# Rotating straight from PSUM, and head pairs' logits in the two row halves of the array, in a two-layer encoder trunk

## The chip, the cores and the metric

The kernel runs on one NeuronCore of a Trainium2 chip. The metric is the device time of one execution in microseconds (us); the profiled times are counted from the first to the last instruction of that core (the span). TensorE (PE in the profile) multiplies, VectorE (DVE) and ScalarE (ACT) work elementwise, GpSimd (POOL) and SyncE (SP) here mostly issue DMAs.

## The reference, cut to what matters

Two layers act on a residual stream of 512 tokens by 1024 channels. Each has a SwiGLU block, a mixer, a second SwiGLU block and a gated embedding. The change lies in the mixer of layer 0, which has two attention groups over keys of the same or earlier chunks of 64 tokens:

```python
aq = apply_rope(rms_norm(aq.reshape(bsz, s_len, A_HEADS, HEAD_DIM), a_q_g), cos, sin)   # 8 heads
ak = apply_rope(rms_norm(ak, a_k_g)[:, :, None], cos, sin)[:, :, 0]
iq = apply_rope(iq.reshape(bsz, s_len, IDX_HEADS, IDX_DIM), cos, sin)                    # 4 index heads
ik = apply_rope(ik[:, :, None], cos, sin)[:, :, 0]
a_out = dsa_attention(aq, ak, av, iq, ik, iw, a_w_uv)     # the best 128 keys of each query, by index score
bq = apply_rope(rms_norm(bq...), cos, sin)                # 4 heads x 2 maps of 64 channels
bk = apply_rope(rms_norm(bk...), cos, sin)
b_out = diff_attention(bq, bk, bv, lam, subln_g, lam_init)  # softmax(map 0) - lam * softmax(map 1)

def apply_rope(x, cos, sin):
    x1, x2 = jnp.split(x, 2, axis=-1)
    return jnp.concatenate([x1 * c - x2 * s, x2 * c + x1 * s], axis=-1)
```

## The kernel before

Activations are kept transposed: a tile has 128 channels on its partitions and the 512 tokens along its free axis, so two heads of 64 channels share a tile. All weight products run as three matmuls of rounded halves (`mm3`, lines 281 to 283, type fp32r); the attention's own products of the second group run as plain fp32 (`mm`, line 276). One `mm` in fp32 is two MATMUL records in the trace, one in fp32r is one.

Instructions are not emitted in program order. Every helper hands `Plan` an engine, a cost in ns, a latency, the tiles it reads and writes, and a priority; `Plan.order` then simulates the engines greedily with these costs and with the number of slots of each pool (`SLOTS`, and `CAPS` for a stream's share; the pair `("ps", "lgpvB")` may hold 2 PSUM banks), and the kernel is emitted in the order that comes out. From there each engine works its list strictly in order and waits where an input is not there. A changed cost thus changes the order on every engine.

The mixer in layer 0 (`even_mixer`) runs from about 385 to 630 us of the span:

- 385 to 440: projections of the index heads and the shared key, rotation of three tiles, index scores (stream `sc`).
- 440 to 487: eight projections for `bqk` (four tiles of `bq`, four of `bk`), each rotated by `rope`; DVE starts to pick the best keys (`max` and `match_replace`, lines 912 and 913).
- 487 to 553: differential attention (stream `pvB`): for each of 4 heads and each of 4 query blocks `t` two logit products over N = 128 (t + 1) keys, then max, exponential, combination, transposes and the product with the values. The projections of `aq` (stream `aq`) fill the gaps on PE, each again rotated.
- 553 to 590: the output projection of that group (`down`), mixed with the start of the sparse attention; 590 to 630: the rest of the sparse attention (stream `pvA`).

`rope_` rotates a tile p (15 tiles in all: 3, then 8, then 4). ACT copies p out of PSUM to zc; four DMAs on SP's queue write the copy with each head's 32-channel halves exchanged to zs; DVE multiplies zc by cos and zs by sin (both with a gain per channel for 13 of the 15 tiles) and adds the two. `halves` makes two zeroed tiles for each `bk` tile (POOL memsets, line 343), into which DMAs put head map 0 in the upper and map 1 in the lower 64 partitions, so that a logit product can run over all 128 partitions with the whole `bq` tile.

Of the kernel before, what the change touches and what calls it, by code (L numbers as in the profile page):

```python
# [257 lines left out]
def trunk(ctx: ExitStack, tc: tile.TileContext, A: dict, out: bass.AP):  # L258
    nc = tc.nc
# [8 lines left out]
    def mm(p, a, b, start, stop):  # L268
        n = b.n
        if a.store.dt == F32R:  # L270
            cost = max(213.0 if n < 256 and n < 192 else 0.0, n * 0.422)
        else:
            cost = 150.0 if a.n <= 64 and n <= 128 else max(n, 127) * 1.68
            if a.arr.shape[0] <= 64:
                cost *= 2
        P.op("PE", cost, lambda: nc.tensor.matmul(ap(p), ap(a), ap(b), start=start, stop=stop), w=[p], r=[a, b], lat=160.0)  # L276

    def mm3(p, a, b, first, last):
# [82 lines left out]
    def tt(dt=F32, shape=(128, S)):  # L361
        return P.tile("t", shape, dt)
# [340 lines left out]
    def vectors():  # L703
        gdma(cst, A["cst"])
        qk = tt(shape=(4, 64))
        for i, name in enumerate(["b_q_g", "b_k_g", "a_q_g", "a_k_g"]):
            gdma(qk[i:i + 1, :], A[name])
        p = ps()
        for j in range(2):
            r = tt(shape=(4, 2, 2, 32))  # L710
            for b in range(2):
                for a in range(2):
                    vcopy(r[:, a, b, :], qk[:, 32 * (b ^ j):32 * (b ^ j) + 32])
            transpose(p[:, 4 * j:4 * j + 4], r.flat(), ident[0:4, 0:4])
        vcopy(vcol[:, 0:8], p[:, 0:8])
        vset(vcol[64:128, 3:4], 1.0)
        vset(vcol[64:128, 7:8], 1.0)
        vrow = tt(shape=(VR - 8, 128))
        gdma(vrow[0:1, :], A["b_subln_g"])
        gdma(vrow[1:9, :], A["c_b_s"][0])  # L720
        for i, name in enumerate(["d_conv_b", "d_ln_g", "d_ln_b"]):
            gdma(vrow[9 + 4 * i:13 + 4 * i, :], A[name].rearrange("e (k p) -> (e k) p", p=128))
        p = ps()
        transpose(p[:, 0:VR - 8], vrow, ident[0:VR - 8, 0:VR - 8])
        vcopy(vcol[:, 8:VR], p[:, 0:VR - 8])
        ts(vcol[:, 8:9], vcol[:, 8:9], 0.8, None, OP.mult)
# [46 lines left out]
    def even_mixer(norm, nxt, cos, sin):  # L773
# [8 lines left out]
                return rope_(*a)  # L782

        def rope_(p, gi, ssq=None):
            zc = tt()
            acopy(zc, p)
            if ssq is not None:
                sq = tt()
                act(sq, p, AF.Square)
                colsums(ssq, sq, ind)  # L790
            zs = tt()
            for b in range(4):
                dma(zs[32 * b:32 * b + 32, :], zc[32 * (b ^ 1):32 * (b ^ 1) + 32, :], 64)
            if gi is None:
                tmul(zc, zc, cos)
                tmul(zs, zs, sin)
            else:
                stt(zc, zc, vcol[:, gi:gi + 1], cos, OP.mult, OP.mult)
                stt(zs, zs, vcol[:, gi + 4:gi + 5], sin, OP.mult, OP.mult)
            dst = at()  # L800
            tadd(dst, zc, zs)
            return dst

        def head_factor(c, R):
# [8 lines left out]
        def stack(x, pool, both):  # L813

            hi, lo = split(x, tt)
            d = [[pool(F32R) for _ in range(2 if both else 1)] for _ in range(2)]
            for c in range(2):
                own = slice(64 * c, 64 * c + 64)
                for b in range(2):
                    half = slice(64 * b, 64 * b + 64)  # L820
                    if both:
                        dma(d[c][0].bitcast(F32)[half, :], hi.bitcast(F32)[own, :], 128)
                        dma(d[c][1].bitcast(F32)[half, :], lo.bitcast(F32)[own, :], 128)
                    else:
                        dma(d[c][0].bitcast(F32)[half, :], (hi, lo)[b].bitcast(F32)[own, :], 128)
            return d

        def halves():
            d = [at(), at()]
            gset(d[0][64:128, :], 0.0)  # L830
            gset(d[1][0:64, :], 0.0)
            return d

        wv = w.rearrange("(k p) c -> p k c", p=128)
# [99 lines left out]
        with P.on("side", SIDE_BIAS):  # L934
            fB = head_factor(rows, 16)
            fq = small(NT, 8)
            ts(fq, fB[:, :, 0:8], 0.125, None, OP.mult)
            bk = []
            for h in range(4):
                fb = bcast2(fB, 8 + 2 * h)  # L940
                d = halves()
                tmul(bqk[4 + h], fb, bqk[4 + h])
                for b in range(2):
                    dma(d[b][64 * b:64 * b + 64, :], bqk[4 + h][64 * b:64 * b + 64, :], 128)
                bk.append(d)

        P.stream = "main"

# [4 lines left out]
        def softmax_exp_(maps, N, bias, fcol):  # L953
            n = len(maps)
            mx, nb, sm = small(n), small(n), small(n)
            es = []
            for i, (q, ks) in enumerate(maps):
                p = ps()
                for j, k in enumerate(ks):
                    mm(p[:, 0:k.n], q, k, j == 0, j == len(ks) - 1)  # L960
                e = tt()
                dve(e[:, 0:N], lambda e=e, p=p, i=i: nc.vector.tensor_tensor_reduce(  # L962
                    out=ap(e[:, 0:N]), in0=ap(p[:, 0:N]), in1=ap(bias), scale=1.0, scalar=LOW,
                    op0=OP.add, op1=OP.max, accum_out=ap(mx[:, i:i + 1])), [p, bias], extra=[mx])
                es.append(e)
            stt(nb, mx, -1.0, fcol, OP.mult, OP.mult)
            for i, e in enumerate(es):
                act(e[:, 0:N], e[:, 0:N], AF.Exp, scale=fcol[:, i:i + 1], bias=nb[:, i:i + 1], accum=sm[:, i:i + 1])
            recip(sm, sm)
            return es, sm  # L970
# [17 lines left out]
        with P.on("pvB"):  # L988
            c = ps((128, NT, 4))
            oc = []  # L990
            for h in range(4):
                po = ps()
                for t in range(NT):
                    N = 128 * (t + 1)
                    (e0, e1), rs = softmax_exp([(bqk[h][:, 128 * t:128 * t + 128], (bk[h][c][:, 0:N],)) for c in range(2)],
                                               N, cmask[:, S - N:S], fq[:, t, 2 * h:2 * h + 2])
                    tmul(rs[:, 1:2], rs[:, 1:2], nlam)
                    scaled(e1[:, 0:N], e1[:, 0:N], rs[:, 1:2])
                    stt(e0[:, 0:N], e0[:, 0:N], rs[:, 0:1], e1[:, 0:N], OP.mult, OP.add)
                    pT = ps()  # L1000
                    for b in range(t + 1):
                        transpose(pT[:, 128 * b:128 * b + 128], e0[:, 128 * b:128 * b + 128], ident)
                    aT = tt()
                    moved(aT[:, 0:N], pT[:, 0:N])
                    for b in range(t + 1):
                        mm(po[:, 128 * t:128 * t + 128], bv[b][:, 128 * h:128 * h + 128],
                           aT[:, 128 * b:128 * b + 128], b == 0, b == t)
# [262 lines left out]
```

## Time and profile before

| what | value |
|---|---|
| median of 3 runs | 2010.78 us (2010.63 to 2011.23) |
| the profiled execution | 2010.54 us, span 2008.6 us |
| PE busy | 1991.3 us of the span, 99% |
| DVE busy / ACT busy / POOL busy | 1080.8 / 723.2 / 13.8 us |
| mean granted clock of PE | 0.999 of 2.4 GHz |

The difference of 1.9 us between time and span lies outside the instructions. A busy PE need not be at its full rate: matmuls overlap, and an instruction that starts late still counts as busy while its predecessor drains. So start times are compared below, not durations.

### The profile page before, as it was taken

The numbers are of one execution on the slowest core, as the hardware profiler recorded it, in microseconds if no ns is written. First come the engines' busy times: TensorE is split into PE (matmuls) and PEld (weight loads), VectorE is DVE, ScalarE is ACT, GpSimd is POOL, SyncE is SP. The second block draws the span as 40 slices with busy tenths as digits, with TensorE's granted clock in tenths as the row PEclk, the third lists the DMA queues.
The fourth block names the chain that finished last, engine by engine and source line by source line (L and its number), as shares of the span: only waits on it lengthen the run. The fifth ranks groups of instructions, "written<-read, shape, count | busy, mean of one in ns | idle before, by whom it ended". The sixth has DMA issues, their size and how long they took to land.

```text
span 2008.6 us, 22735 instructions
## 1 busy us (share of the span) xinstructions
PE 1991.3 (99%) x9154; PEld 1630.2 (81%) x9154; DVE 1080.8 (54%) x1797; ACT 723.2 (36%) x1057; POOL 13.8 (1%) x35
## 2 busy tenths in 40 slices
PE   8999999999999999999999999999999999999999
PEld 7888888888767888888888888888767888888887
DVE  6442464489986544344466443444699744334443
ACT  6322233344756422132254222223425533213232
POOL 0000000000000000000000000000000000000000
PEclk9999999999999999999999999999999999999999
DMA  5323322354330323332233322323333232323222
GB/s 189 105 97 98 108 85 84 94 160 141 96 110 22 104 86 105 94 95 95 95 121 110 105 98 92 105 75 103 107 105 105 84 97 92 105 85 104 95 104 75
DMA packets 164778, 202.28 MB, mean 101 GB/s; under 512 B 9968, under 2 KB 123072, under 8 KB 164672
## 3 DMA queue, kind: packets, MB, share of 16 engines
q1 hardware_dynamic: 164016, 200.38, 31.3%
q8 instruction: 72, 1.18, 0.2%
q0 software_dynamic: 528, 0.41, 0.2%
q14 instruction: 34, 0.28, 0.0%
q10 hardware_dynamic: 128, 0.03, 0.0%
HBM read 185.33 MB, written 6.29 MB: 95 GB/s over the span
## 4 chain that ended last, share of the span: by engine, by line
PE 97%; DVE 1%; ACT 1%; DMA 1%; issue 0%; SPq 0%; ACTq 0%; DVEq 0%
PE ps L281 30%; PE ps L282 30%; PE ps L283 30%; PE ps L276 6%; PE ps L287 1%; DMA whi<-in_x_dram 0%; ACT t L292 0%; ACT t L297 0%; DVE t L962 0%; DVE t L330 0%; DVE wlo L330 0%; DMA t<-t 0%; DVE t L309 0%; DVE wlo L321 0%; DVE a L913 0%
## 5 line engine op out<-in xcount | busy, mean ns | idle before, releaser
L297 ACT CAST whi<-raw 128x1024 fp32r<-128x1024 f32 (+2 forms) x342 | 348.7, 1022 | 976.3 <-PE ps L282 936.7
L321 DVE TENSOR_TENSOR wlo<-raw,whi 128x1024 fp32r<-128x1024 f32 (+2 forms) x342 | 405.1, 1185 | 496.8 <-ACT whi L297 496.0
L281 PE MATMUL ps<-x,whi 128*128 128x512 f32 x1664 | 655.8, 394 | 0.6 <-ACT x L297 0.6
L282 PE MATMUL ps<-x,whi 128*128 128x512 f32 x1664 | 648.7, 390 | 0.6 <-DVE x L321 0.6
L283 PE MATMUL ps<-x,wlo 128*128 128x512 f32 x1664 | 648.8, 390 | 0.0
L281 PEld LDWEIGHTS ps<-x,whi 128*128 128x128 f32 x1664 | 313.1, 188 | 66.2 <-ACT x L297 1.1
L283 PEld LDWEIGHTS ps<-x,wlo 128*128 128x128 f32 x1664 | 312.9, 188 | 65.6
L282 PEld LDWEIGHTS ps<-x,whi 128*128 128x128 f32 x1664 | 313.2, 188 | 65.1 <-DVE x L321 1.2
L281 PE MATMUL ps<-a,whi 128*128 128x512 f32 x832 | 325.1, 391 | 0.0
L282 PE MATMUL ps<-a,whi 128*128 128x512 f32 x832 | 323.9, 389 | 0.0
L283 PE MATMUL ps<-a,wlo 128*128 128x512 f32 x832 | 323.8, 389 | 0.0
L281 PEld LDWEIGHTS ps<-a,whi 128*128 128x128 f32 x832 | 156.3, 188 | 32.8 <-issue 0.5
L283 PEld LDWEIGHTS ps<-a,wlo 128*128 128x128 f32 x832 | 156.2, 188 | 32.6
L282 PEld LDWEIGHTS ps<-a,whi 128*128 128x128 f32 x832 | 156.2, 188 | 32.3 <-DVE a L321 0.7
L315 DVE TENSOR_TENSOR t<-ps,t 128x512 f32<-128x512 f32 x88 | 60.8, 691 | 209.1 <-PE ps L283 208.3
L315 DVE TENSOR_TENSOR t<-ps,rb 128x512 f32<-128x512 f32 x100 | 68.7, 687 | 112.1 <-PE ps L283 109.9
L330 DVE SCALAR_TENSOR_TENSOR a<-a 128x508 f32<-128x508 f32 (+23 forms) x108 | 72.7, 731 | 5.0 <-ACT a L292 4.6
L292 ACT ACTIVATE t<-t 128x512 f32<-128x512 f32 x100 | 62.9, 629 | 22.9 <-DVE t L315 22.8
L297 ACT CAST a<-t 128x512 fp32r<-128x512 f32 x88 | 54.8, 623 | 36.8 <-DVE t L315 36.8
L315 DVE TENSOR_TENSOR t<-t,rb 128x512 f32<-128x512 f32 x92 | 63.2, 687 | 1.2
L321 DVE TENSOR_TENSOR a<-t,a 128x512 fp32r<-128x512 f32 x88 | 60.4, 686 | 5.2 <-ACT a L297 4.8
L276 PE MATMUL ps<-a 128*128 128x512 f32 (+3 forms) x152 | 58.6, 501 | 1.5 <-ACT t L297 0.5
(167 smaller groups left out, 1358.8 us busy)
## 6 DMA issues: line engine op xcount, KB each, us to landing
raw<-in_ffn_wg_dram SPq DMA_DIRECT2D x43, 1024.0 KB, 5.1
raw<-in_ffn_wu_dram SPq DMA_DIRECT2D x43, 1024.0 KB, 5.1
raw<-in_ffn_wd_dram SPq DMA_DIRECT2D x40, 1024.0 KB, 4.9
raw<-in_ple_wgate_dram SPq DMA_DIRECT2D x8, 1024.0 KB, 5.0
raw<-in_od_w_in_dram SPq DMA_DIRECT2D x8, 1024.0 KB, 5.5
raw<-in_ev_w_in_dram SPq DMA_DIRECT2D x7, 1024.0 KB, 5.8
raw<-in_ffn_wd_dram SPq DMA_DIRECT2D x8, 512.0 KB, 3.7
raw<-in_ev_w_out_dram SPq DMA_DIRECT2D x4, 1024.0 KB, 5.3
```

Source lines behind the costliest of these rows:

```text
L276: P.op("PE", cost, lambda: nc.tensor.matmul(ap(p), ap(a), ap(b), start=start, stop=stop), w=[p], r=[a, b], lat=160.0)
L281: nc.tensor.matmul(q, x, u, start=first, stop=False)
L282: nc.tensor.matmul(q, x, v, start=False, stop=False)
L283: return nc.tensor.matmul(q, y, u, start=False, stop=last)
L287: P.op("PE", 107.0, lambda: nc.tensor.transpose(ap(p), ap(x), ap(idn)), w=[p], r=[x, idn], lat=160.0)
L292: P.op("ACT", cost, lambda: nc.scalar.activation(ap(o), ap(x), func, scale=ap(scale), bias=ap(bias), **({"accum_out": ap(accum)} if accum ...
L297: P.op("ACT", 0.83 * o.n + (52.0 if x.psum else 93.0), lambda: nc.scalar.copy(ap(o), ap(x)), w=[o], r=[x])
L315: dve(o, lambda: nc.vector.tensor_mul(ap(o), ap(a), ap(b)), [a, b])
L321: dve(o, lambda: nc.vector.tensor_sub(ap(o), ap(a), ap(b)), [a, b])
L330: dve(o, lambda: nc.vector.scalar_tensor_tensor(ap(o), ap(a), ap(s), ap(b), op0=op0, op1=op1, **kw()), [a, s, b], extra=[accum] if accum i ...
```

## The change

`rope_` no longer copies p. DVE multiplies p, still in PSUM, once by sin (into zs) and once by cos (into the result), and four DMAs on POOL's queue add the 32-row pieces of zs, exchanged, into the result (`accum_op`). Since the product with sin is now taken at the neighbour's row, the sign of sin and the gain are those of that row; the second set of four gain columns goes. `halves` and its DMAs go: `bk` is two views of the rotated tile's 64 partitions, and a logit product takes 64 partitions of `bq` and of `bk` (map 0: partitions 0 to 63, map 1: 64 to 127). `softmax_exp_` issues the products of both maps ahead of the first max. The planner's cost of an fp32 product over 64 partitions or fewer becomes half of a full one plus 45 ns; no product of before was of that kind.

```diff
@@ mm
             cost = 150.0 if a.n <= 64 and n <= 128 else max(n, 127) * 1.68
             if a.arr.shape[0] <= 64:
-                cost *= 2
+                cost = cost / 2 + 45.0
@@ vectors
-        for j in range(2):
-            r = tt(shape=(4, 2, 2, 32))
-            for b in range(2):
-                for a in range(2):
-                    vcopy(r[:, a, b, :], qk[:, 32 * (b ^ j):32 * (b ^ j) + 32])
-            transpose(p[:, 4 * j:4 * j + 4], r.flat(), ident[0:4, 0:4])
-        vcopy(vcol[:, 0:8], p[:, 0:8])
+        r = tt(shape=(4, 2, 64))
+        for b in range(2):
+            vcopy(r[:, b, :], qk)
+        transpose(p[:, 0:4], r.flat(), ident[0:4, 0:4])
+        vcopy(vcol[:, 0:4], p[:, 0:4])
@@ rope_
-            zc = tt()
-            acopy(zc, p)
             if ssq is not None:
                 sq = tt()
                 act(sq, p, AF.Square)
                 colsums(ssq, sq, ind)
-            zs = tt()
+            dst, zs = at(), tt()
+            if gi is None:
+                tmul(zs, p, sin)
+                tmul(dst, p, cos)
+            else:
+                stt(zs, p, vcol[:, gi:gi + 1], sin, OP.mult, OP.mult)
+                stt(dst, p, vcol[:, gi:gi + 1], cos, OP.mult, OP.mult)
             for b in range(4):
-                dma(zs[32 * b:32 * b + 32, :], zc[32 * (b ^ 1):32 * (b ^ 1) + 32, :], 64)
-            if gi is None:
-                tmul(zc, zc, cos)
-                tmul(zs, zs, sin)
-            else:
-                stt(zc, zc, vcol[:, gi:gi + 1], cos, OP.mult, OP.mult)
-                stt(zs, zs, vcol[:, gi + 4:gi + 5], sin, OP.mult, OP.mult)
-            dst = at()
-            tadd(dst, zc, zs)
+                P.op("POOL", 1000.0, lambda o=dst[32 * b:32 * b + 32, :], x=zs[32 * (b ^ 1):32 * (b ^ 1) + 32, :]:
+                     nc.gpsimd.dma_start(ap(o), ap(x), accum_op=OP.add), w=[dst], r=[zs], lat=2500.0)
             return dst
@@ even_mixer
-                d = halves()
                 tmul(bqk[4 + h], fb, bqk[4 + h])
-                for b in range(2):
-                    dma(d[b][64 * b:64 * b + 64, :], bqk[4 + h][64 * b:64 * b + 64, :], 128)
-                bk.append(d)
+                bk.append([bqk[4 + h][64 * b:64 * b + 64, :] for b in range(2)])
@@ softmax_exp_
-            for i, (q, ks) in enumerate(maps):
-                p = ps()
+            logits = [ps() for _ in maps]
+            for p, (q, ks) in zip(logits, maps):
                 for j, k in enumerate(ks):
                     mm(p[:, 0:k.n], q, k, j == 0, j == len(ks) - 1)
+            for i, p in enumerate(logits):
                 e = tt()
@@ even_mixer, pvB
-                    (e0, e1), rs = softmax_exp([(bqk[h][:, 128 * t:128 * t + 128], (bk[h][c][:, 0:N],)) for c in range(2)],
+                    (e0, e1), rs = softmax_exp([(bqk[h][64 * c:64 * c + 64, 128 * t:128 * t + 128], (bk[h][c][:, 0:N],)) for c in range(2)],
                                                N, cmask[:, S - N:S], fq[:, t, 2 * h:2 * h + 2])
```

What this does to the engines' lists is seen in three places. In the rows, `ps<-a 128xN` is a logit product (`a` holds queries and keys, N keys), `ident,t` a transpose, `t,a 128x128` the product with the values, and the three rows with `x,whi` or `x,wlo` are one `mm3` of a projection. First PE, the third of the four heads of the differential attention, blocks t = 1 to 3, before the change:

```order
L276 MATMUL ps<-a 128x256 x2
L276 MATMUL ps<-t,a 128x128
L287 MATMUL ps<-ident,t 128x128 x5
L281 MATMUL ps<-x,whi 128x512
L282 MATMUL ps<-x,whi 128x512
L283 MATMUL ps<-x,wlo 128x512
L276 MATMUL ps<-a 128x384 x2
L276 MATMUL ps<-t,a 128x128 x5
L276 MATMUL ps<-a 128x512 x2
L287 MATMUL ps<-ident,t 128x128 x5
```

The same head on PE with the change, blocks t = 2 and 3 (line numbers are one higher there):

```order
L277 MATMUL ps<-a 128x384
L277 MATMUL ps<-t,a 128x128 x2
L288 MATMUL ps<-ident,t 128x128 x3
L277 MATMUL ps<-a 128x384
L282 MATMUL ps<-x,whi 128x512
L283 MATMUL ps<-x,whi 128x512
L284 MATMUL ps<-x,wlo 128x512
L277 MATMUL ps<-t,a 128x128 x2
L277 MATMUL ps<-a 128x512
L277 MATMUL ps<-t,a 128x128
L288 MATMUL ps<-ident,t 128x128 x3
L277 MATMUL ps<-a 128x512
```

The two products of a pair stood side by side and now stand apart, with products and transposes over all 128 partitions between them. Over the 4 heads and 4 blocks the list of PE has 8 of the 16 pairs side by side before and 4 with the change (N = 128, 384 and 512 of the first head, N = 512 of the last). In the first head, with the change, they stand so:

```order
L277 MATMUL ps<-a 128x128 x2
L282 MATMUL ps<-x,whi 128x512
L283 MATMUL ps<-x,whi 128x512
L284 MATMUL ps<-x,wlo 128x512
L288 MATMUL ps<-ident,t 128x128 x4
L277 MATMUL ps<-a 128x256
L282 MATMUL ps<-x,whi 128x512
L283 MATMUL ps<-x,whi 128x512
L284 MATMUL ps<-x,wlo 128x512
L288 MATMUL ps<-ident,t 128x128 x4
L277 MATMUL ps<-a 128x256
```

So the 32 products over 64 partitions make 28 separate groups on PE. From the second block of the sparse attention (about 587 us) on, PE's list is the same as before.

The third place is POOL, from the last constant that it loads to its last memsets; before:

```order
L350 DMA t<-in_b_lam_k_dram 128x64
L350 DMA t<-in_b_lam_q_dram 128x64
L350 DMA t<-in_b_lam_k_dram 128x64
L343 MEMSET a 64x512 x8
L343 MEMSET whi 128x1
```

With the change:

```order
L351 DMA t<-in_b_lam_k_dram 128x64
L351 DMA t<-in_b_lam_q_dram 128x64
L351 DMA t<-in_b_lam_k_dram 128x64
L797 DMA a<-t 32x512 x60
L344 MEMSET whi 128x1
```

POOL loses eight memsets and gains 60 DMAs; SP's list loses as many (`t<-t 32x512`) and the eight `a<-a 64x512` of `halves`.

## Rows read from the trace of the kernel before

**Rows 1.** The page: busy time by engine, and the chain that ended last.

```profile
PE 1991.3 (99%) x9154; PEld 1630.2 (81%) x9154; DVE 1080.8 (54%) x1797; ACT 723.2 (36%) x1057; POOL 13.8 (1%) x35
...
PE 97%; DVE 1%; ACT 1%; DMA 1%; issue 0%; SPq 0%; ACTq 0%; DVEq 0%
```

**Rows 2.** Stretches: length, busy PE, PEld, DVE, ACT, POOL, clock, DMA, GB/s.

```profile
420.00:440.00 20.00, 19.56 (x97) 15.23 (x95) 16.62 (x37) 11.85 (x25) 3.29 (x6) 1.00 0.43 114
...
487.00:553.00 66.00, 64.65 (x364) 49.79 (x363) 64.21 (x218) 47.09 (x110) 0.52 (x1) 1.00 0.41 113
...
590.00:630.00 40.00, 35.56 (x261) 27.13 (x260) 29.38 (x104) 29.56 (x78) 0.00 (x0) 1.00 0.11 34
```

**Rows 3.** PE in order of time, logit products: start, length, form, records.

```profile
519.30 1.88 PE L276 MATMUL ps<-a 128*128 128x512 f32 x4
521.02 0.71 PE L287 MATMUL ps<-ident,t 128*128 128x128 f32 x5
...
522.96 0.61 PE L276 MATMUL ps<-a 128*128 128x128 f32 x4
523.40 1.06 PE L276 MATMUL ps<-t,a 128*128 128x128 f32 x8
```

**Rows 4.** PE in order of time around a transpose of 48, then of 124 rows.

```profile
18.05 0.39 PE L283 MATMUL ps<-x,wlo 128*128 128x512 f32 x1
18.37 0.26 PE L287 MATMUL ps<-ident,t 48*128 48x48 f32 x1
...
18.90 0.39 PE L282 MATMUL ps<-x,whi 128*128 128x512 f32 x1
...
1429.92 0.39 PE L283 MATMUL ps<-x,wlo 128*128 128x512 f32 x1
1430.15 0.27 PE L287 MATMUL ps<-ident,t 124*128 124x124 f32 x1
...
1430.49 0.39 PE L282 MATMUL ps<-x,whi 128*128 128x512 f32 x1
```

**Rows 5.** PE in order of time around products into 64 columns (128*64).

```profile
574.53 0.43 PE L276 MATMUL ps<-t,a 128*64 128x128 f32 x2
...
575.92 0.40 PE L283 MATMUL ps<-a,wlo 128*128 128x512 f32 x1
576.25 0.44 PE L276 MATMUL ps<-t,a 128*64 128x128 f32 x4
...
576.95 0.40 PE L282 MATMUL ps<-a,whi 128*128 128x512 f32 x1
577.19 0.39 PE L283 MATMUL ps<-a,wlo 128*128 128x512 f32 x1
```

**Rows 6.** DVE and ACT groups, 385 to 600 us: form, count, busy, mean ns.

```profile
L330 DVE SCALAR_TENSOR_TENSOR t<-t,vcol,cs 128x512 f32<-128x512 f32 x26 | 18.7, 744 | 3.3 <-DMA t<-t 3.3
L318 DVE TENSOR_TENSOR a<-t 128x512 f32<-128x512 f32 x15 | 10.3, 684 | 0.0
L330 DVE SCALAR_TENSOR_TENSOR a<-a,vcol,ps 128x512 f32<-128x512 f32 x4 | 2.8, 745 | 0.0
L297 ACT COPY t<-ps 128x512 f32<-128x512 f32 x27 | 15.5, 586 | 44.4 <-PE ps L283 37.6 <-PE ps L276 6.9
```

**Rows 7.** POOL in order of time, one DMA issue: start, length.

```profile
241.02 0.54 POOL L350 DMA_DIRECT2D t<-in_b_lam_q_dram  x1 [96.52 <-DVE t L334]
```

**Rows 8.** DMA issues by kind: count, KB each, us to landing.

```profile
t<-t SPq DMA_DIRECT2D x60, 64.0 KB, 2.0
...
t<-in_pos_dram POOLq DMA_DIRECT2D x1, 256.0 KB, 3.6
```

**Rows 9.** The first rotations in order of time: first copy, last sum, first scores.

```profile
394.90 0.59 ACT L297 COPY t<-ps 128x512 f32<-128x512 f32 x1 [2.27 <-PE ps L283]
...
407.42 0.69 DVE L318 TENSOR_TENSOR a<-t 128x512 f32<-128x512 f32 x1
...
422.45 0.73 PE L276 MATMUL ps<-a 128*128 128x256 f32 x4 [0.44 <-PE ps L283]
```

More of the change, by code (lines that the diff above doesn't have):

```diff
@@ L708, in vectors @@
         p = ps()
-        for j in range(2):
-            r = tt(shape=(4, 2, 2, 32))
-            for b in range(2):
-                for a in range(2):
-                    vcopy(r[:, a, b, :], qk[:, 32 * (b ^ j):32 * (b ^ j) + 32])
-            transpose(p[:, 4 * j:4 * j + 4], r.flat(), ident[0:4, 0:4])
-        vcopy(vcol[:, 0:8], p[:, 0:8])
+        r = tt(shape=(4, 2, 64))
[3 more added lines that the diff above has]
+        vcopy(vcol[:, 0:4], p[:, 0:4])
         vset(vcol[64:128, 3:4], 1.0)
-        vset(vcol[64:128, 7:8], 1.0)
         vrow = tt(shape=(VR - 8, 128))
@@ L825, in stack @@
                         dma(d[c][0].bitcast(F32)[half, :], (hi, lo)[b].bitcast(F32)[own, :], 128)
[L826 to L831, printed above, removed]
             return d
@@ L1259 @@
     cst[:, 0] = _np.tile(inv, 4)
-    cst[:, 1] = _np.tile(_np.repeat(_np.float32([-1.0, 1.0]), 32), 2)
+    cst[:, 1] = _np.tile(_np.repeat(_np.float32([1.0, -1.0]), 32), 2)
     host["cst"] = cst
```

## The prediction

> **What bounds the kernel now.** I read the page first: PE is busy for 99% of the span and holds 97% of the chain that ended last [rows 1]. The reader is to see that a change on any other engine moves the end only through a wait of PE, and that a change in PE's own work moves it one for one. Then I cut the mixer into stretches [rows 2]. From 487 to 553 us, where the changed logit products run, PE is busy 64.65 of 66.0 us and DVE 64.21: both are full, PE sits idle for 1.35 us. From 420 to 440 it sits idle for 0.44. Only in the last stretch, 590 to 630, are there 4.44 us of idle PE, and there its list does not change. So whatever waiting the change can remove is at most 1.35 + 0.44 = 1.8 us. The rest must come from PE's work, and for that I read PE in order of time, start to start.
>
> **What the logit products cost now.** Four records with 512 keys take 519.30 to 521.02, 0.43 us each, and four with 128 keys 522.96 to 523.40, 0.11 each [rows 3]. A product is two records, so it takes 0.22 us with 128 keys and 0.86 with 512, and by the straight line between 0.43 with 256 and 0.65 with 384. Eight products of each size make 8 x 2.16 = 17.3 us.
>
> **What two halves of the array do.** The trace of before has no product over 64 partitions, but it has the same thing across columns: the product with the values in the sparse attention fills 64 columns. Two such records, one product, take 0.43 us, four records, two products for the two halves, 0.44 [rows 5]. So two halves do run beside each other when they stand side by side, and the second product of a pair is then free. That is what I take for rows. Only 4 of the 16 pairs stand side by side in the new list; their second products are worth 0.22 + 0.65 + 0.86 + 0.86 = 2.6 us. The other 12 pairs have work over all 128 partitions between their halves and save nothing, since a product over 64 partitions still streams as many keys. The Trainium skill (TensorE: Matmul & The Clock Gate, Part 3, What overlaps and what doesn't) says that matmuls start and end strictly in program order; by that, the second product could start only beside the first one's second record, and 1.3 us would be saved. The trace disagrees for columns (four records in the time of two), so I keep 2.6; strict order is a rival below.
>
> **What changing over costs.** This is the term that decides, and no row shows it directly. Two rows are near. A transpose of 48 rows uses part of the array's rows: from the start of the record before it to the start of the second one behind it 18.05 to 18.90 = 0.85 us pass, with a transpose of 124 rows 1429.92 to 1430.49 = 0.57 [rows 4]. The smaller one is dearer by 0.28. And around the two products in column halves 575.92 to 576.95 = 1.03 us pass; the projection records at its ends take 0.23 and 0.24 when alone (576.95 to 577.19), the four records 4 x 0.11 / 2 = 0.22, which leaves 0.34 [rows 5]. Of this the way in shows alone in 18.05 to 18.37, 0.32 in place of 0.23: 0.09 [rows 4]. So a visit to a half-array shape costs between 0.09 us (if the way out were hidden) and 0.34; nothing is excluded, since both ways show a loss wherever the shape changes. I take 0.31, the middle of the two complete visits. The new list makes 28 visits: 24 lone products and 4 pairs. 28 x 0.31 = 8.7 us, where the planner has put 45 ns on each product and counted each as half.
>
> **The rotation.** DVE keeps 30 products and loses 15 sums (10.3 us). A product that reads PSUM costs what one from SBUF does: 745 against 744 ns [rows 6]. ACT loses 15 of its 27 copies of this form, 15 x 0.586 = 8.8 us [rows 6]. Neither engine is the last to end, so this is worth only the waits of PE that it removes. Of the 1.8 us I take 1.2: PE will be later than its plan by the visits, so more of its inputs will be there. The way through POOL: an issue takes 0.54 us there [rows 7], landing is 2.0 us for the 64 KB pieces on SP's queue and 3.6 for 256 KB on POOL's [rows 8]. What an accumulating transfer takes no row shows; I bound it by these two. For the first three tiles the work now goes from ACT's first copy at 394.90 to the end of DVE's last sum at 408.11 [rows 9]. With the change six products end at 394.9 + 6 x 0.745 = 399.4, twelve issues from 396.4 on end at 402.9, and the last landing is at 404.9 to 406.5, so not later than now; SP's queue is free sooner for what follows. The later tiles come one in some 6 us (eight in 440 to 487) and need 4 x 0.54 = 2.2 us of POOL, which does nothing else: hidden, and worth nothing. The products hold a PSUM bank until DVE has run both, 1.5 us, where the copy let it go after 0.59 [rows 9]; should PE miss a bank for that, it shows as a new wait, at most 0.9 us for each of 15 tiles, which I count at nothing because the new lists keep one projection's matmuls (24 records of 0.23 us, 5.5 us) between two rotated tiles.
>
> **Small edits.** The memsets on POOL and the eight DMAs of the zeroed halves lay beside PE's work; they wait for nothing that PE waits for, except that the first logits now follow the product with the head factor directly: counted in the 1.2. One 4-row transpose less: 0.1 us.
>
> **The sum**, on the profiled execution's own 2010.5 us (the median of the runs shown is 2010.8): + 8.7 - 2.6 - 1.2 - 0.1 = + 4.8, so 2015.3 us. What differs by less than 0.2% (4.0 us) cannot be told from no change here: from 2006.8 to 2014.8 counts as the same.
>
> **Rivals.**
> - *Changing over is cheap*: 0.09 to 0.26 us a visit, the drain hidden behind waits that PE has anyway. With the 2.6, 0.1 and up to 1.8 us of waits taken off, 2010.5 + 2.5 - 4.5 = 2008.5 at one end, 2010.5 + 7.3 - 3.9 = 2013.9 at the other. For it: logits often follow a wait of PE. Against: PE's idle time of that stretch is 1.35 us in all. The same time within 0.2%.
> - *All pairs overlap* (the other side: faster). If PE pulls a half's records ahead past work over the whole array, all second products are free: 17.3 / 2 = 8.65 us saved; with visits then for 16 pairs, 16 x 0.31 = 5.0, it is 2010.5 - 8.65 + 5.0 - 1.2 - 0.1 = 2005.5. It decides once 12 of the 16 pairs overlap. The Trainium skill (TensorEngine Tiling, Theoretical Speedup) gives up to twice the speed for 64 rows; by that alone 17.3 would become 8.65. Against: in the rows only halves of one shape run beside each other [rows 5].
> - *The additions land late.* If an issue of an accumulating DMA takes over (408.1 - 396.4 - 3.6) / 12 = 0.68 us, the last of the first three tiles is later than now, and the scores, which already wait 0.44 us at 422.45 [rows 9], wait by 1.2 us for each 0.1 us above that. With 1.0 us an issue: 3.8 us, 2019.1 in all. For it: DVE is full in this time, and no row shows such a transfer. Against: 0.54 us.
> - *Strict order between halves*: 1.3 us saved in place of 2.6, 2016.6.
>
> **Chances.** The forecast's case, 0.26 to 0.34 us a visit, spans 2013.9 to 2016.1: 0.50, three fifths of it beyond 2014.8. Cheap changing: 0.22. All pairs: 0.07. Late additions: 0.13. Strict order: 0.08. Slower: 0.30 + 0.13 + 0.08 = 0.51; the same: 0.20 + 0.22 = 0.42; faster: 0.07. The range runs from 2008.5, the cheapest visits, to 2010.5 + 28 x 0.34 = 2020.0, the dearest with nothing saved; it leaves out the case of all pairs and the worst of the late additions, 0.13. Without the rivals, 2013 to 2017.
>
> **What will show it.** Start to start on PE: 0.32 to 0.34 us from the record before a logit product over 64 rows where 0.23 stood, and again behind it; the four pairs that stand side by side with their two products at one start, as near as a row shows; lone ones 0.86 us long with 512 keys. POOL with 60 issues of about 0.54 us. DVE idle for some 10 us more between 385 and 590, and 590 to 630 as it was, only later. The prediction is wrong if lone products stream faster than 0.43 us a record, if the records behind them start without a gap, or if PE waits for DMAs of POOL.

## The result, and the profile after

The changed kernel takes 2037.3 us (median of 4 runs, 2032.7 to 2042.2), 1.0132 [1.0103, 1.0161] times the time before: 26.5 us slower, where 4.8 us were predicted and 2020.0 was the end of the range. The profiled execution took 2040.69 us. Its page says that PE is busy for as large a share of the span as it was, 99% [rows 1], and, in the row of the clock's tenths, that one slice is no longer full (its mean over the span is 0.993, 0.999 before):

```profile
span 2038.9 us, 22667 instructions
PE 2012.3 (99%) x9153; PEld 1635.7 (80%) x9153; DVE 1075.3 (53%) x1778; ACT 717.6 (35%) x1039; POOL 57.0 (3%) x87
PEclk9999999999899999999999999999999999999999
PE 96%; DVE 2%; DMA 1%; ACT 1%; issue 0%; SPq 0%; ACTq 0%; DVEq 0%
```

Where the time went is read from windows. Columns: stretch and its length, busy time (and instructions) of PE, PEld, DVE, ACT, POOL, then the granted clock as a share of 2.4 GHz, and DMA. The first row of each kernel is the mixer from the first product of its norm to the first projection of the next block. Before:

```profile
381.72:628.84 247.12, 240.89 (x1385) 192.11 (x1383) 206.89 (x615) 138.16 (x308) 4.33 (x8) 1.00 0.39 113
...
553.00:590.00 37.00, 37.00 (x173) 25.75 (x172) 32.34 (x103) 20.46 (x51) 0.00 (x0) 1.00 0.33 112
```

After, with the stretches that answer to [rows 2]:

```profile
382.96:657.27 274.31, 259.52 (x1385) 195.70 (x1383) 201.37 (x603) 131.07 (x290) 47.44 (x60) 0.96 0.40 98
...
420.00:440.00 20.00, 18.16 (x87) 14.08 (x86) 13.90 (x29) 11.43 (x22) 5.87 (x8) 1.00 0.64 141
440.00:487.00 47.00, 45.12 (x265) 38.98 (x264) 42.40 (x110) 12.09 (x20) 19.42 (x25) 1.00 0.57 117
487.00:553.00 66.00, 63.79 (x254) 40.09 (x253) 45.96 (x165) 32.52 (x78) 6.29 (x8) 0.84 0.25 72
502.00:506.00 4.00, 4.00 (x13) 3.35 (x14) 3.76 (x15) 2.44 (x7) 0.24 (x1) 0.57 0.55 135
506.00:515.00 9.00, 9.00 (x40) 5.04 (x38) 5.98 (x25) 4.08 (x11) 0.00 (x0) 1.00 0.00 0
515.00:523.00 8.00, 8.00 (x45) 5.86 (x45) 5.88 (x21) 5.06 (x10) 0.00 (x0) 0.98 0.01 2
523.00:540.00 17.00, 17.00 (x40) 9.68 (x39) 8.63 (x32) 5.89 (x17) 3.14 (x4) 0.51 0.33 78
553.00:590.00 37.00, 33.03 (x170) 22.78 (x169) 30.45 (x90) 19.31 (x39) 6.29 (x8) 1.00 0.54 139
```

The mixer is 274.3 - 247.1 = 27.2 us longer, of 30.3 us by which the span grew. (Of the rest, the mixer starts 1.2 us later, and near 1590 us a stretch at the lower clock costs some 1.7 us more than the one near 1565 us before.) The 27.2 us split in three. **Idle**: length less PE's busy time is 14.8 us, 6.2 before, so 8.6 more; the row of 553 to 590 alone, where PE was busy throughout before, has 4.0. **Clock**: from 502 to 506 and from 523 to 540 PE runs at 1.2 GHz, the lower of its two levels, with no idle time in either row; in narrow windows it is there for 20.5 us, which loses half, 10.2 us. **Work**: the rest, 27.2 - 8.6 - 10.2 = 8.4 us, is PE's own list taking longer. The same split is made for every run below; idle time at the lower clock is counted in both of the first two, so that the work comes out a little low where there is any.

PE in order of time (start, busy, instruction), the changed kernel. First pairs side by side and lone products, then, from just ahead of the long fall, products with one column, and matmuls at the lower clock:

```profile
491.14 0.49 PE L277 MATMUL ps<-a 64*128 64x128 f32 x4
...
498.26 1.13 PE L277 MATMUL ps<-a 64*128 64x512 f32 x4
...
509.93 0.40 PE L284 MATMUL ps<-x,wlo 128*128 128x512 f32 x1
510.25 0.91 PE L277 MATMUL ps<-a 64*128 64x384 f32 x2
511.09 0.55 PE L288 MATMUL ps<-ident,t 128*128 128x128 f32 x3
511.39 0.47 PE L282 MATMUL ps<-x,whi 128*128 128x512 f32 x1
...
514.30 1.12 PE L277 MATMUL ps<-a 64*128 64x512 f32 x2
515.35 0.33 PE L288 MATMUL ps<-ident,t 128*128 128x128 f32 x1
...
522.04 1.25 PE L277 MATMUL ps<-ones,t 128*128 128x1 f32 x8
...
525.27 0.63 PE L283 MATMUL ps<-x,whi 128*128 128x512 f32 x1
525.70 0.63 PE L284 MATMUL ps<-x,wlo 128*128 128x512 f32 x1
```

Four records with 512 keys at 498.26 take 1.13 us, as the two of the lone product at 514.30 take 1.12: the halves do run beside each other. A lone product with 512 keys takes 514.30 to 515.35 = 1.05 us where 0.86 was forecast. And 525.27 to 525.70 is 0.43 us for a record that takes 0.23 at the full clock.

What PE waits for from 385 to 660 us (engine, output, line, releaser; us in total, times, longest):

```profile
PE ps L288 <- DVE s L316: 2.8, 1, 2.8
PE ps L277 <- ACT t L293: 2.5, 6, 0.7
PE ps L277 <- DMA t<-in_a_w_uv_dram: 1.8, 1, 1.8
PE ps L288 <- DVE t L326: 1.8, 3, 1.0
PE ps L277 <- DVE t L310: 1.7, 4, 0.8
PE ps L277 <- ACT t L298: 1.4, 2, 1.0
PE ps L288 <- DVE t L331: 1.4, 1, 1.4
```

The additions on POOL, its timeline and SP's queue's, for the first three tiles:

```profile
398.89 9.57 POOL L797 DMA_DIRECT2D a<-t  x12 [159.29 <-PE ps L283]
...
410.99 2.44 SPq L347 DMA_DIRECT2D a<-t  x4
...
422.63 0.55 SPq L347 DMA_DIRECT2D t<-in_a_w_uv_dram  x1
```

And their row in the changed kernel's list of DMAs (KB each, median us from issue to landing):

```profile
a<-t POOLq DMA_DIRECT2D x60, 64.0 KB, 3.8
```

An issue takes 9.57 / 12 = 0.80 us, above the 0.68 at which the rival on late additions decides. The DMAs that need the rotated tiles, and the load of `a_w_uv` queued behind them on SP, go late; PE waits 1.8 us for that load. Before, it went 3.3 us earlier:

```profile
419.29 0.59 SPq L346 DMA_DIRECT2D t<-in_a_w_uv_dram  x1
```

### The profile page after: what moved, and what is told of

It is laid out like the page before. It is cut to its first block, busy times and chain, and to the rows that moved or that the text cites. A ratio compares the mean times of both kernels' runs of the same rounds, so it can differ in the third digit from the quotient of the medians.

```text
span 2038.9 us, 22667 instructions
## 1 busy us (share of the span) xinstructions
PE 2012.3 (99%) x9153; PEld 1635.7 (80%) x9153; DVE 1075.3 (53%) x1778; ACT 717.6 (35%) x1039; POOL 57.0 (3%) x87
## 4 chain that ended last, share of the span: by engine, by line
PE 96%; DVE 2%; DMA 1%; ACT 1%; issue 0%; SPq 0%; ACTq 0%; DVEq 0%
PE ps L282 29%; PE ps L283 29%; PE ps L284 29%; PE ps L277 6%; PE ps L288 2%; ACT t L293 0%; DVE a L903 0%; DMA whi<-in_x_dram 0%; DVE m L902 0%; DMA pp<-t 0%; DVE a L331 0%; DVE t L950 0%; DVE wlo L331 0%; ACT t L298 0%; DVE wlo L322 0%
## 5 line engine op out<-in xcount | busy, mean ns | idle before, releaser
L277 PE MATMUL ps<-a 128*128 128x512 f32 (+6 forms) x152 | 61.8, 534 | 0.5 <-ACT t L298 0.5
```

## The experiments

Ratios are to the kernel before on the same chip, with 95% intervals. The first table gives them all; the last three columns split the mixer's added length, in us, as above.

| run | ratio | mixer | idle | clock | work |
|---|---|---|---|---|---|
| changed kernel | 1.0132 [1.0103, 1.0161] | +27.2 | +8.6 | +10.2 | +8.4 |
| e1 rotation only | 1.0058 [1.0042, 1.0074] | +13.7 | +7.2 | +5.1 | +1.5 |
| e2 logits only | 1.0134 [1.0119, 1.0149] | +26.5 | +7.1 | +13.7 | +5.8 |
| e3 changed, full rows | 1.0061 [1.0046, 1.0076] | +10.4 | +8.5 | 0 | +1.9 |
| g1 first three by SP | 1.0045 [1.0030, 1.0060] | +12.6 | +8.0 | +1.7 | +2.9 |
| g2 exchange by SP | 1.0035 [1.0022, 1.0048] | +7.4 | +3.2 | +1.7 | +2.4 |
| g3 logits only, full rows | 1.0080 [1.0065, 1.0095] | +18.3 | +7.6 | +10.2 | +0.5 |
| c1 list only | 1.0032 [1.0021, 1.0043] | +6.1 | +1.9 | +1.7 | +2.5 |
| c2 list only | 1.0058 [1.0045, 1.0072] | +11.4 | +3.9 | +5.1 | +2.4 |
| c3 list only | 1.0030 [1.0018, 1.0042] | +9.0 | +2.8 | +5.1 | +1.1 |
| k3 row halves, old list | 1.0018 [1.0010, 1.0027] | +5.1 | -0.2 | +1.7 | +3.7 |
| k4 five pairs, old list | 0.9998 [0.9989, 1.0007] | +1.8 | +1.1 | +1.7 | -1.0 |
| h1 row halves, full price | 1.0038 [1.0023, 1.0053] | +9.5 | -0.2 | +1.7 | +8.1 |
| h3 changed, true prices | 1.0124 [1.0091, 1.0157] | +19.8 | +7.2 | +10.2 | +2.4 |
| e4 pairs together | 1.0013 [1.0004, 1.0023] | +1.8 | +0.9 | 0 | +0.9 |
| h4 pairs, full price | 1.0062 [1.0047, 1.0077] | +13.9 | +7.9 | +6.8 | -0.8 |
| g4 pairs, mixed rotation | 1.0027 [1.0016, 1.0037] | +6.5 | +5.4 | +1.7 | -0.6 |

The split is of one profiled execution each; the ratio is of several, whose mean clock differs (two of the changed kernel's four had 0.996 and spans of 2030.9 and 2032.0 us; e3's had 0.998 three times and 0.996 once; e1's 0.996 and 0.999, twice each). The kernel before has 0.997 to 1.000 over its own runs, so 1.7 us in the column of the clock says nothing of an edit. c3's split is of the slowest of its five executions, 2021.1 us, where the others had 2013.8 to 2018.4.

### One half of the change at a time

e1 keeps the new rotation and takes the old logits; e2 the reverse. Each is the change's diff with the other half's lines left out.

> The new rotation alone; the logits as before, over 128 partitions with zeroed halves. Theory A (the row halves cost most, by changes of shape and by the clock that falls among them): the rotation costs only what its later additions delay, 2013 to 2017 us, and the clock stays at its upper level from 487 to 560 us (mean clock 0.999). Theory B (the additions through POOL come late, PE waits, and the clock falls because of these waits): 2025 to 2037 us, with a stretch at half clock in the mixer.

> The logits in row halves alone, with the planner's new cost; the rotation as before. Theory A: 2026 to 2034 us, with stretches at half clock between 490 and 560 us and about 0.35 us for each visit to the half shape. Theory B: 2011 to 2016 us, only the visits, and the mean clock stays at 0.999.

2022.7 and 2038.2 us. Each half alone costs far more than its term, the two do not add up, and in e2, which has no accumulating DMA, the clock falls for longer than in the changed kernel. e1 lies between its theories, e2 4 us above its theory A. In e1, too, PE waits 1.5 us for the load of `a_w_uv`.

### Is it the row halves, or the list?

e3 is the changed kernel with the same lists on all engines, but each logit product reads all 128 partitions (so it gives the sum of both maps' logits). g3 does the same to e2.

```diff
-(bqk[h][64 * c:64 * c + 64, 128 * t:128 * t + 128], (bk[h][c][:, 0:N],))
+(View(bqk[h].store, bqk[h][64 * c:64 * c + 64, 128 * t:128 * t + 128].arr, bqk[h][:, 128 * t:128 * t + 128].steps),
+ (View(bqk[4 + h].store, bk[h][c][:, 0:N].arr, bqk[4 + h][:, 0:N].steps),))
```

The planner goes by the view's `arr`, which stays that of a half; PE reads by `steps`, the whole tile.

> The changed kernel with the same order on every engine, but each logit product is taken over all 128 partitions of the two tiles (so a logit holds the sum of both maps: part of the computation is changed, the instructions and their order are not). Theory A: the 28 visits (28 x 0.35 = 9.8 less 2.6 for the pairs) and the half clock go: 2014 to 2021 us. Theory B: the waits and the clock stay: 2030 to 2037 us.

> The old rotation; the list of the run with the new logits alone, but each logit product runs over all 128 partitions (it so gives the sum of both maps' logits, in place of one map's). Theory A (the array's row halves themselves are dear, by their visits and by the clock they bring down): 2009 to 2014 us, no stretch below 0.99 of the clock in the mixer. Theory B (the new list, ordered with a halved price for these products, is dear): 2022 to 2032 us.

2022.9 and 2028.3 us. e3 lies 2 us above its theory A, far below B. In its profiled execution the clock holds throughout the mixer. Its windows, the mixer and two of the stretches above:

```profile
382.19:639.72 257.53, 242.83 (x1385) 192.13 (x1383) 200.67 (x603) 130.82 (x290) 47.42 (x60) 1.00 0.42 104
515.00:523.00 8.00, 7.81 (x48) 6.66 (x48) 7.50 (x30) 6.62 (x16) 3.15 (x4) 1.00 0.48 87
523.00:540.00 17.00, 16.12 (x92) 12.16 (x90) 14.51 (x51) 11.74 (x30) 0.00 (x0) 1.00 0.15 52
```

And PE in order of time, where e3 stands at the changed kernel's 509.93 of above:

```profile
505.92 0.40 PE L284 MATMUL ps<-x,wlo 128*128 128x512 f32 x1
506.15 0.81 PE L277 MATMUL ps<-a 128*128 128x384 f32 x2
506.79 0.49 PE L288 MATMUL ps<-ident,t 128*128 128x128 f32 x3
507.04 0.48 PE L282 MATMUL ps<-x,whi 128*128 128x512 f32 x1
```

The same four steps of the list take 505.92 to 507.04 = 1.12 us here and 509.93 to 511.39 = 1.46 with row halves: a visit costs 0.34 us. The Trainium skill (TensorEngine Tiling, Key Properties) says that changing the tiling mode drains the engine; the trace agrees as far as each visit loses time, with that number. Between the changed kernel and e3 the mixer differs by 27.2 - 10.4 = 16.8 us: 0.1 of idle time, 6.5 of work and 10.2 of clock. So in this list, and in the executions profiled, the clock falls with the row halves and holds without them.

In g3's list they are not needed: with full rows the clock falls all the same. Its windows:

```profile
525.00:530.00 5.00, 4.58 (x20) 2.99 (x19) 4.15 (x18) 2.69 (x7) 0.00 (x0) 1.00 0.41 147
530.00:535.00 5.00, 1.15 (x4) 0.30 (x2) 4.99 (x15) 3.67 (x9) 0.00 (x0) 0.87 0.22 52
535.00:550.00 15.00, 14.09 (x52) 11.99 (x53) 10.83 (x39) 8.86 (x20) 0.00 (x0) 0.50 0.39 106
```

Ahead of the fall PE is busy for 1.15 of 5 us. In this list the projections of `aq`, which fill PE's waits for the softmax, are used up too soon (their last row starts at 525.7, before at 546.3), and PE stands still. So theory B of g3 held: the list alone makes most of e2's loss, 18.3 of 26.5 us in the mixer.

### The list alone

c1, c2 and c3 compute exactly what the kernel before computes, with the same instructions. Only the planner's price of the rotation's 15 copies is changed, by +60, +100 and -100 ns, and with it the order in the mixer.

```diff
-            acopy(zc, p)
+            P.op("ACT", 0.83 * p.n + 112.0, lambda: nc.scalar.copy(ap(zc), ap(p)), w=[zc], r=[p])
```

> A control: the kernel before with the same instructions, only the planner prices the 15 copies of the rotation 60 ns dearer, and so puts about a tenth of the mixer's instructions elsewhere in the engines' lists. Theory A (the list of before is an unusually good one, and any other greedy list brings new waits of PE, whatever the change computes): 2014 to 2022 us. Theory B (a list that is only shuffled costs nothing, so the time comes from the changed instructions): 2009 to 2013 us.

> A control like the first one: the instructions of the kernel before, the planner's price of the rotation's 15 copies 100 ns higher. Theory A (another list costs): 2013 to 2024 us. Theory B (it costs nothing): 2009 to 2013 us.

> A third control: the instructions of the kernel before, the planner's price of the rotation's 15 copies 100 ns lower, which moves about half as many rows as the other two. Theory A (another list costs, less where less moves): 2011 to 2018 us. Theory B (it costs nothing): 2009 to 2012 us.

2017.1, 2022.4 and 2016.0 us. All three are theory A's. These three lists, which are only shuffled, cost 0.30 to 0.58%, more than was predicted for the whole change; that every other list would cost is not shown by three. c2 brings the clock down with no new instruction at all; its windows show PE idle for 1.81 of 5 us ahead of the fall:

```profile
565.00:570.00 5.00, 3.19 (x23) 2.49 (x21) 5.00 (x15) 4.43 (x10) 0.00 (x0) 0.98 0.30 108
570.00:577.00 7.00, 6.82 (x21) 3.82 (x21) 6.08 (x23) 4.68 (x16) 0.00 (x0) 0.53 0.00 0
```

### The row halves alone

k3 keeps the lists of before row for row, the zeroed copies of the keys too, and only lets each logit product read 64 partitions; k4 does so for the five pairs of two 384- or 512-key products that already stand side by side.

```diff
+        def half(x, c, lo, hi):
+            return View(x.store, x[:, lo:hi].arr, x[64 * c:64 * c + 64, lo:hi].steps)
...
-(bqk[h][:, 128 * t:128 * t + 128], (bk[h][c][:, 0:N],))
+(half(bqk[h], c, 128 * t, 128 * t + 128), (half(bk[h][c], c, 0, N),))
```

> The kernel before, its lists on all engines unchanged row for row (the zeroed copies and their DMAs too); each of the 32 logit products now really reads 64 partitions. In that list 8 of the 16 pairs stand side by side. Theory A (row halves cost a visit of 0.35 us and save a second product where a pair stands together, no more): 24 x 0.35 - (0.22 + 2 x 0.43 + 2 x 0.65 + 3 x 0.86) = 8.4 - 5.0 = 3.4 us, so 2012.5 to 2016 us, the clock as before. Theory B (the visits empty the array so often that the clock falls in 487 to 553 even without the holes of another list): 2019 us or more, with half clock there.

> The same list again; only the five pairs that stand side by side in it with 384 or 512 keys read 64 partitions, all other logit products all 128. Theory A: 5 x 0.35 - (2 x 0.65 + 3 x 0.86) = 1.75 - 3.9 = -2.1 us on PE, of which DVE, full in this stretch, may leave nothing: 2008.4 to 2011 us. Theory B (row halves are dear in themselves): 2013 us or more.

k3: 2015.0 us against 2011.5, + 3.5 us (2.0 to 5.4 by the interval), where 3.4 was worked out from visits and pairs: theory A. Its windows:

```profile
381.62:633.88 252.26, 246.27 (x1384) 189.32 (x1382) 207.34 (x615) 138.60 (x308) 4.33 (x8) 0.99 0.38 111
487.00:553.00 66.00, 65.12 (x346) 43.87 (x346) 61.41 (x209) 45.05 (x106) 0.52 (x1) 1.00 0.39 110
```

There are 23 visits in 487 to 553 (one product joins the pair behind it), and the clock stays at 1.00: in the old list, which has few holes, the row halves do not bring it down. (The 1.7 us of clock in the table are lost near 600 us, where k4 and h1 lose them too.) k4 gains nothing: PE has 1.0 us less work, where 2.1 was expected, and 1.1 us more idle time. Standing side by side in the list is not enough for a pair, as two of k4's five show:

```profile
517.11 1.24 PE L276 MATMUL ps<-a 64*128 64x384 f32 x4
519.59 1.13 PE L276 MATMUL ps<-a 64*128 64x512 f32 x4
```

The one with 384 keys takes longer than the one with 512, since its second product starts later; so it is with three of the five, and with two of k3's eight. In the changed kernel, too, the second product of the pair at 558.11 comes late. Its weight load waits for a copy out of PSUM by DVE, so probably for the bank that this copy frees:

```profile
558.67 0.29 PEld L277 LDWEIGHTS ps<-a 64*128 64x128 f32 x2 [0.26 <-DVE t L310]
```

Two further runs, k1 and k2, meant for the same question as k3 and k4, read all 128 partitions and so repeated the kernel before: 1.0002 [0.9993, 1.0011] and 1.0000 [0.9991, 1.0008], which is what such a comparison resolves.

### The rotation's way

g1 sends the neighbour's part of the first three tiles through four DMAs on SP's queue and a sum on DVE, g2 that of all 15; the products stay straight from PSUM, the logits are the old ones. g2's edit, which g1 makes for the first three tiles alone:

```diff
-            for b in range(4):
-                P.op("POOL", 1000.0, lambda o=dst[32 * b:32 * b + 32, :], x=zs[32 * (b ^ 1):32 * (b ^ 1) + 32, :]:
-                     nc.gpsimd.dma_start(ap(o), ap(x), accum_op=OP.add), w=[dst], r=[zs], lat=2500.0)
+            zx = tt()
+            for b in range(4):
+                dma(zx[32 * b:32 * b + 32, :], zs[32 * (b ^ 1):32 * (b ^ 1) + 32, :], 64)
+            tadd(dst, dst, zx)
```

> The old logits; all 15 tiles rotated by two products straight from PSUM, but for the first three (the shared key and the two index tiles) the neighbour's part is exchanged by four DMAs on SP's queue and added by DVE; for the other 12 tiles POOL's accumulating DMAs add it. Theory A (the late first additions cost: POOL's twelve issues of 0.80 us end at 408.5 and hold up the index scores and what stands behind them on SP's queue): most of the 12 us that the rotation alone cost comes back, 2011 to 2015 us, and the first index score stands within 1.5 us of where it stood before. Theory B (it is the later 12 tiles, whose additions or PSUM banks come late): little changes, 2019 to 2024 us.

> The old logits; all 15 tiles rotated by two products straight from PSUM, the neighbour's part exchanged by four DMAs on SP's queue and added by DVE: no accumulating DMA at all, only ACT's copies are gone and DVE holds the PSUM bank for its two products. Theory A (the way through POOL is what costs): 2009 to 2013 us. Theory B (what costs is that the products take longer to free the PSUM bank, and that DVE, which is full, now stands ahead of the exchange): 2016 to 2024 us, with PE waiting for DVE's products in 385 to 487.

2021.2 and 2018.3 us, against 2022.7 for e1. The first index score starts at 421.42 in g1 and 420.98 in g2, 428.80 in e1 and 422.45 before [rows 9]; e1's row, then g1's:

```profile
428.80 1.11 PE L276 MATMUL ps<-a 128*128 128x256 f32 x8
...
421.42 1.10 PE L276 MATMUL ps<-a 128*128 128x256 f32 x4 [1.92 <-issue]
```

So the late additions are real and g1 removes them. But g1 gives back only 1.5 us, less than the intervals tell apart; by its time it is theory B's. g2, without POOL, has theory B's time too, but not its sign: the one wait of PE for DVE in 385 to 487, 1.6 us, is for a copy between two tiles and not for a product of the rotation.

```profile
409.40 0.42 DVE L334 COPY t<-s 128x512 f32<-128x512 f32 x1
...
409.87 0.65 PE L287 MATMUL ps<-ident,t 128*128 128x128 f32 x4 [1.56 <-DVE t L334]
```

And 0.35% is what a list costs that is only shuffled, so that products holding PSUM longer are not shown to cost anything.

### Mending

h1 is the old rotation and order of a pair's maps, with row halves priced as full products and no zeroed copies. h3 is the changed kernel with the planner's numbers set to what its trace shows:

```diff
             if a.arr.shape[0] <= 64:
-                cost = cost / 2 + 45.0
+                cost += 330.0
...
-                P.op("POOL", 1000.0, lambda o=dst[32 * b:32 * b + 32, :], x=zs[32 * (b ^ 1):32 * (b ^ 1) + 32, :]:
-                     nc.gpsimd.dma_start(ap(o), ap(x), accum_op=OP.add), w=[dst], r=[zs], lat=2500.0)
+                P.op("POOL", 800.0, lambda o=dst[32 * b:32 * b + 32, :], x=zs[32 * (b ^ 1):32 * (b ^ 1) + 32, :]:
+                     nc.gpsimd.dma_start(ap(o), ap(x), accum_op=OP.add), w=[dst], r=[zs], lat=3800.0)
```

e4 and h4, both with the old rotation, plan a pair of products as one step, e4 with the price below and four banks, h4 with that of two full products and the two banks of before; g4 is e4's pairs with g1's rotation:

```diff
+                def pair(jobs=[(p, q, ks[0]) for p, (q, ks) in zip(logits, maps)]):
+                    for p, q, k in jobs:
+                        r = nc.tensor.matmul(ap(p[:, 0:k.n]), ap(q), ap(k), start=True, stop=True)
+                    return r
+                P.op("PE", max(N, 127) * 2.0 + 350.0, pair, w=logits, r=[v for q, ks in maps for v in (q, ks[0])], lat=160.0)
```

> The old rotation and the old order of a pair's two maps, but each logit product over 64 partitions and no zeroed copies of the keys; the planner's price of such a product stays that of a full one. Theory A (the fall of the clock in the run with the new logits came from the holes that the halved price put into PE's list; the row halves themselves cost only their visits, 0.35 us each, less what pairs side by side save): 2013 to 2020 us, no stretch below 0.99 of the clock in 487 to 590. Theory B (products over half the rows bring the clock down by themselves): 2024 to 2036 us with half clock in that stretch.

> The changed kernel with the planner's numbers taken from its own trace: a logit product over 64 partitions at the price of a full one plus 330 ns, an accumulating DMA at 800 ns an issue and 3800 ns to landing. Theory A (wrong prices make the list of after wait): 2016 to 2026 us, with PE idle less than 5 us in 487 to 590 and no half clock there. Theory B (the change is dear under any list): 2032 to 2042 us.

> The rotation as before; the logits in row halves, with both products of a pair handed to the planner as one operation (2.0 ns a key and 350 ns), so that all 16 pairs stand side by side (four PSUM banks for them instead of two). If only lone products lose: 16 visits of 0.35 us = 5.6, 8.6 saved, 2007 to 2010 us at a mean clock of 0.999. If half-array products as such let the clock fall: 2015 to 2025 us with a stretch at half clock.

> The old rotation; each pair of logit products over 64 partitions as one step of the plan, side by side on PE, priced as two full products and with the two PSUM banks of before. By the trace of the changed kernel a pair costs one product's time and one visit, 16 x 0.35 = 5.6 us against 17.3 / 2 = 8.7 us saved, so 2007 to 2011 us if the list is no worse than that of before (theory A); 2013 to 2020 us if the wait for both banks at once and another list eat it (theory B).

> Each pair of logit products over 64 partitions as one step of the plan, side by side on PE, with four PSUM banks for that stream; all tiles rotated by two products straight from PSUM, the first three with exchange on SP's queue and a sum on DVE, the others with accumulating DMAs on POOL's queue. Theory A (both halves of the change are harmless once the pairs stand together and the first additions don't pass POOL): 2004 to 2012 us. Theory B (POOL's additions of the later tiles are late as well, or DVE bounds this stretch): 2013 to 2022 us.

2019.1, 2033.6, 2014.0, 2023.3 and 2017.4 us. With the full price (h1) PE waits no more than before and the clock holds from 487 to 590: theory A. Of its 8.1 us of work some 6 are visits (an estimate: 26 x 0.34 less the 2.7 that its pairs save); the other 2 are of the size that a shuffled list adds. True prices (h3) repair little, theory B: its runs, 2029.9 to 2044.3 us, cannot be told from the changed kernel's, and idle time and clock stay, so wrong prices alone do not explain a list that waits. e4 lies between its theories; its pairs start together, and yet its work is 0.9 us more than before, where visits and pairs alone would make it 3.0 less. h4 lies above both of its theories: PE waits 7.9 us more, and whether the price or the two banks for both maps at once does it is not told apart. g4 is within theory B. Pairs kept together come to 0.13% above before at best; no version here beats it.

## Why the prediction was wrong, point by point

- **The visits: right.** 0.31 us each was taken, 0.34 is measured; 28 x 0.31 - 2.6 = 6.1 us forecast, 6.5 us of work between the changed kernel and e3. In the old list the sum at 0.35 a visit gives 3.4, and k3 shows 3.5; that close an agreement is partly luck, since k3 has one visit less than was counted and two of its pairs do not start together. The way in is 0.32, as in [rows 4]; part of the price lies in the product's first record, 0.53 us and not 0.43 (514.30 to 515.35 is 1.05). Three of the four pairs start together; the fourth has its halves 0.55 us apart, since the second waits for a copy out of PSUM.
- **The waits: the step that failed first.** "Of the 1.8 us I take 1.2", because a later PE would find more of its inputs there. The 1.8 us bound what a change can take away; nothing bounded what a new list can add, and that was put at nothing. PE's idle time rose by 8.6 us in place of falling by 1.2. The lists are new on every engine, and three lists that differ by a price alone brought 1.9 to 3.9 us of idle time. A kernel whose PE is idle for 6 us in this stretch has little to win by another order and much to lose; the prediction had no term for that.
- **The clock: the other failed step, a term left out.** 10.2 us. No rival named it, though the time stood on a clock of 0.999. Ahead of a fall two things were seen: PE standing still (g3, 3.85 of 5 us; c2, 1.81 of 5), and, in the changed kernel, a stretch without a hole: PE is busy for 9.00 of 9.00 and 8.00 of 8.00 us ahead of its longest fall, with eight visits in them. That the visits are needed in this list is shown by e3, which has none and keeps the clock in 487 to 553. That they are not enough is shown by k3, which has eight visits in as many us (505.9 to 523) and keeps it too, as does h1. What in the changed list has to come to them stays open.
- **The rotation, "not later than now" for the first three tiles: wrong in its sizes.** 0.54 us an issue was taken from another transfer, 0.80 is measured, 3.1 us more for twelve, and the first issue comes 2.5 us later than taken; so the twelfth ends at 408.5 and not 402.9. SP's queue is not "free sooner": the load behind these DMAs goes 3.3 us later. The rival on late additions had the mechanism and the deciding point right. Its price, 1.2 us for each 0.1 above 0.68, would be 1.4 us; PE waits 1.8, for that load and not, as the rival had it, at the scores. What of e1's 0.58% is more than this stays open, since a list alone gives the same.
- **The rivals.** Cheap visits and all pairs overlapping are excluded by the rows at 510.25 and by the lone products of 1.05 us. (By its own prices the second would have counted as faster from 14 pairs on (the widest first), at 2006.6 us, and not from 12.) Strict order is excluded by the pair at 498.26: had the second product started only beside the first one's second record, four records would have taken half as long again.
- **Open**: the 1 to 2.5 us of work that a shuffled list adds, and which waits of the new list follow from which moved row; the longest, 2.8 us for `s` in 553 to 590, among them.

## What to carry to other kernels

Where a greedy planner writes the lists, a changed price or instruction is two changes, and the second, the new list, can be the larger one, as it was here: run a control that has the new list and the old instructions, or the old list and the new instructions, before a term is put down to the instruction. Where PE is 99% busy, cost the idle time that a new list may bring, and the clock that goes with it, as a term with its own bounds. Halves of the array can pay only if their products start together: a lone visit costs 0.34 us and saves nothing, and standing side by side in the list does not yet make a pair start together. That they pay at all is shown by no run here.

## What the runs showed of the hardware

Busy time in the profile does not tell whether the clock holds: PE was busy for 8.00 of 8.00 us ahead of its longest fall, with row halves, and for 7.81 in the same 8 us of e3, where the clock stayed. Two fp32 products in the two row halves take the time of one if both can start (four records with 512 keys 1.13 us, two 1.12). An accumulating DMA from one tile to another costs POOL 0.80 us an issue and lands after 3.8 us (median of 60), against 2.0 us for a plain one of the same size on SP's queue [rows 8].
